# A DiT layer, from its first norm to its feed-forward: a fourth up tile in the norm's freed PSUM banks, and a written order of convolutions and operands

## The chip, the cores and the metric

The kernel runs on one core of a Trainium2 chip (trn2). The metric is the device time of one execution in microseconds (us), from the first to the last instruction of the core; where a number of runs is given, it is their median. Engines are named as in the profile: PE is TensorE's matmul (PEld its weight loads), DVE is VectorE, ACT is ScalarE, POOL is GpSimd, SP is SyncE, which here only issues DMAs (SPq).

## The reference, cut to what matters

One layer of a diffusion backbone over 1024 latent tokens and 256 context tokens, model width 1024, in fp32. Two attentions are merged, then comes a norm, then a feed-forward with a depthwise convolution of width 3 along the tokens, then a second norm. The change lies between the first norm and the feed-forward:

```python
x = _layer_norm(DEEPNORM_ALPHA * x + gate1 * y, ln1_g[l], ln1_b[l])
h = x * (1.0 + scale2) + shift2
y = _conv_ffn(h, w_up[l], conv_w[l], conv_b[l], w_down[l])
x = _layer_norm(DEEPNORM_ALPHA * x + gate2 * y, ln2_g[l], ln2_b[l])

def _conv_ffn(h, w_up, conv_w, conv_b, w_down):
    u = h @ w_up                      # 1024 -> 2 * 2816
    u = depthwise_conv3(u, conv_w) + conv_b
    gate, val = jnp.split(u, 2, axis=-1)
    return (jax.nn.silu(gate) * val) @ w_down
```

## The kernel before, in words

Activations lie transposed: 128 channels on the partitions, the tokens along the row. Every fp32 operand is split into a high part (a cast, on ScalarE) and a low part (the remainder, on VectorE or GpSimd), and a product is three matmuls: high-high, high-low, low-high (`mm3`, L87 to L90). `split` is L77 to L85; so nearly all casts show as L80 and nearly all weight remainders as L85, and `sub`'s differences as L1074.

**The first norm** works in three token ranges, `LN1_S`: tokens 0 to 511, 512 to 767, 768 to 1023. For each range `ln_steps` sums over the channels with small matmuls into a PSUM tile `sml`, spreads the result with another, and then, per channel block f of eight, applies it (L1050, L1052) and calls `emit1`: an affine step on ScalarE into the operand tile `B{f}_{half}` (its high part) and into a full value v, and the remainder into B's low part. B is the moving operand of the feed-forward's first matmuls.

**PSUM** has eight banks of 512 fp32 words per partition. The pool `ps3` has three `big` tiles of two banks each (1024 tokens) and two `sml` tiles of one bank. A pool is replaced by the next one bank by bank, as their readers end.

**The up tiles.** The 2816 + 2816 columns are 22 tiles j, each with a gate half (gv 0) and a value half (gv 1) of 128 channels. The first NCL = 3 tiles are direct products: u{gv}_{j} is 8 channel blocks x 3 matmuls x the tokens (`up_mm`, L1259 on). Tiles 3 to 21 use a form with seven products of half size (`up_tile`): A11, S2, S1, S3, A12, S4, A22, each 4 x 3 matmuls of 512 columns, with sums of the weights (`wsums`, GpSimd) and of the activations (`build`) as operands. `build(k)`, for k of 0 to 3, makes differences t13, t24 of the values (VectorE and GpSimd) and splits them into T13 and T24, high and low. `prods` says which product uses which: S2 needs T2 and A22 T4, both from T24; S1 and S3 need T1 and T3 from T13; A11, A12 and S4 use B itself.

**A direct tile's end.** `conv3` (L1229 on) convolves one half from PSUM into SBUF: a scaled copy on ScalarE (L1230), two shifted multiply-adds on VectorE (L1231, L1233); only then are the two banks free. Then silu of the gate half (L1283, ScalarE) and `gated`: a product (L1242) and an add (L1243) on VectorE, and stores to DRAM (`td`) on the SP queue (L1244 to L1246). The gate half c0 lies in one of two fixed slots `cs`; the value half c1 takes a slot from the free list.

**The free list.** `ht` takes the first slot of `hfree`, `hput` appends slots to its end, at the moment at which the program text is traced; the wait for the slot's last reader, a DMA included, becomes a wait of the instruction that writes the new tile first.

**The order.** TensorE is in an order written by hand (`tc.manual_schedule` over PE, entered ahead of this part and left at the kernel's end). The other engines' orders are chosen by the language's scheduler, by the order of the text among what its own model finds ready. Small steps are queued in `pend` with a due time and called by `tick` between matmuls; `drain` calls the rest.

Before the change three tiles (0,0), (0,1), (1,0) start in the three `big` buffers, range by range behind the norm (L1289 to L1296). Then the 16 steps of the four builds are put into `pend` at 2400 each, `up_conv(0)`, `up_conv(1)`, `up_conv(2)` follow (the missing half of tile 1 and both of tile 2 take a `big` buffer as one comes free), `drain` calls what is left of the builds, and the pool is replaced by `ps3u` with eight single banks. `up_tile(3)` takes four of them in the order of `PSU`.

Of the kernel before, what the change touches and what calls it, by code (L numbers as in the profile page):

```python
# [7 lines left out]
F32 = mybir.dt.float32  # L8
# [30 lines left out]
LN2_D = 5000.0, 4000.0, 2500.0, 1500.0, 700.0  # L39
LN2_E = 3500.0, 3000.0, 1500.0, 800.0, 500.0  # L40
NCL = 3
BLD = 2400.0
LN2_S = slice(0, 512), slice(512, 768), slice(768, 1024)
S1 = 0, 1
KVB = 2
# [22 lines left out]
def layer_kernel(  # L68
# [66 lines left out]
    def hput(*names):  # L135
        for n in names:
            hfree.append(hslot.pop(n))
# [735 lines left out]
    za = tc.alloc_tile_pool(name="za", bufs=1, side="right", reuse_waits="tile")  # L873
    wq = tc.alloc_tile_pool(name="wq", bufs=1, side="right", reuse_waits="tile")
    ps3 = tc.alloc_tile_pool(name="ps3", bufs=1, space=PSUM, reuse_waits="tile")

    hfree += [(za, f"Z{n}") for n in range(16)]

# [4 lines left out]
        return ps3.tile([P, T], F32, tag="big", name=name, bufs=3)  # L883

    def sml(name, w=512):
        return ps3.tile([P, w], F32, tag="sml", name=name, bufs=2)

    def weight(src, nm, n=8, tag="w", he=None, le=None, rtag="raw"):
        if rtag:
# [215 lines left out]
    def build(k):  # L1105
        (b11, b21), (b12, b22) = [[z[:, a] for a in (0, 1)] for z in (zt_[k, 0], tp["v", k])]
        st = {}

        def parts(a, e):
            for p in "hl":  # L1110
                tp[a + p, k] = ht(f"T{a}{p}_{k}", (P, 2, HALF), R32)
            nc.scalar.copy(tp[a + "h", k], st[a])
# [12 lines left out]

        return [s1, s2, lambda: parts("13", nc.vector), lambda: parts("24", nc.vector)]
# [145 lines left out]
    def up_conv(j):  # L1272
        cv = []
        for gv in (0, 1):
            up_mm(j, gv, [hsl(0), hsl(1)])
            if gv == 0:
                hslot[f"c0_{j}"] = pool, tag = cs[j % 2]
                t = pool.tile([P, T], F32, tag=tag, name=f"c0_{j}", bufs=1)
            else:
                t = ht(f"c1_{j}")  # L1280
            conv3(t, ups.pop((j, gv))[0], gv * NF + j)
            cv.append(t)
        nc.scalar.activation(cv[0], cv[0], AF.Silu)  # L1283
        gated(j, *cv)
        hput(f"c1_{j}")

    up_weights(1, 0, 1)
    up_weights(1, 1, 1)
    for j, gv in ((0, 0), (0, 1), (1, 0)):  # L1289
        up_start(j, gv)  # L1290
    for si, s in enumerate(LN1_S):
        drain((len(LN1_S) - 1 - si) * (KT + 3))
        for j, gv in ((0, 0), (0, 1), (1, 0)):
            up_mm(j, gv, [s])
            if s.stop == T:
                ups[j, gv][2].add(HALF)  # L1296
    cs = [hfree.pop(0) for _ in range(2)]
# [5 lines left out]
    hput(*[f"B{k}_1" for k in range(4)])  # L1303


    ps3.release()
    ps3 = tc.alloc_tile_pool(name="ps3u", bufs=1, space=PSUM, reuse_waits="tile")

    ubanks = list(PSU)

    def bank(name):
        n = ubanks.pop(0)
        ubanks.append(n)
        return ps3.tile([P, HALF], F32, tag=f"u{n}", name=name)

    for n in range(8):
        ps3.tile([P, HALF], F32, tag=f"u{n}", name=f"u{n}")

    def wload(j):
        wraw[j] = [post.tile([P, 8, P], F32, tag="raw", name=f"ru{gv}_{j}", bufs=3) for gv in (0, 1)]  # L1320
        for gv in (0, 1):
            nc.sync.dma_start(wraw[j][gv], w_up[2 * j + gv])
# [13 lines left out]
    def pairs(j, *names):  # L1336
        for n in names:
            if (j, n) not in wsrc:
                continue
            pool, tag = ((wq, "w"), (post, "wd"))[npair[0] % 2]  # L1340
            npair[0] += 1
            t = wtile[j, n] = pool.tile([P, 2, HALF], R32, tag=tag, name=f"w{n}_{j}", bufs=4)
            split(wsrc.pop((j, n)), t[:, 0], t[:, 1], nc.scalar, getattr(nc, UE[list(prods).index(n)]))

    def prod(j, n, o, start, stop):
        w = wtile.pop((j, n))
        for k in range(4):
            c = slice(k * P, (k + 1) * P)
            mm3(o, (w[:, 0, c], w[:, 1, c]), opnd(prods[n], k), start and k == 0, stop and k == 3, not start)
            tick(HALF / 0.8)  # L1350

    def add(o, p, q, e=nc.vector):
        e.tensor_tensor(out=o, in0=p, in1=q, op=ALU.add)

    lohalf, hihalf = slice(0, HALF), slice(HALF, T)

    def up_tile(j):
# [7 lines left out]
        nc.scalar.copy(pe, a)  # L1365
# [368 lines left out]
```

## Time and profile before

| | |
|---|---|
| median of 3 runs | 1618.45 us (1617.1 to 1619.27) |
| the profiled execution: span | 1618.4 us |
| TensorE busy (matmuls) | 1545.6 us, 95% |
| VectorE / ScalarE / GpSimd busy | 1199.0 / 816.8 / 746.4 us |
| mean granted TensorE clock | 0.987 |
| the stretch from 949.3 to 1029.0 us | 79.7 us, TensorE busy 67.07, clock 0.89 |

The profiled execution's own time is its span; nothing else lies around it. A row of the windows gives a stretch and, for each engine, busy time and number of instructions, then the clock that TensorE was granted. A row of the waits reads "who waited, at which tile and line, <- for what: total us, times, longest". In order of time a row is start, length, engine, line, operation, out<-in, and, in brackets, idle time of the engine before it and what ended it. Matmuls are pipelined: their listed lengths overlap, and the distance between starts is what one costs.

### The profile page before, as it was taken

To read this page: it belongs to the slowest core of one execution; us is meant where nothing else is said; L and a number is where in the kernel's file an instruction comes from. 1 tells how busy PE (TensorE), PEld (TensorE's weight loads), DVE (VectorE), ACT (ScalarE), POOL (GpSimd) and SP (SyncE) were. 2 spreads that over 40 slices of the span, in tenths; PEclk is the share of its full clock that TensorE was granted. 3 is DMA by queue.
4 is the path that set the end of the run, shared out by engine and by line. 5 is a ranking of instruction groups with operands and counts; after the bars stand their busy time and mean duration, and the time that the engine had idled before them with its cause. 6 is when DMAs were issued, how large, how long until landed. Compare 5 with 4: busy or idle time off the path is not lost.

```text
span 1618.4 us, 22204 instructions
## 1 busy us (share of the span) xinstructions
PE 1545.6 (95%) x7748; PEld 1283.5 (79%) x7748; DVE 1199.0 (74%) x1764; ACT 816.8 (50%) x1455; POOL 746.4 (46%) x731
## 2 busy tenths in 40 slices
PE   6999999999999999999999988999999999999987
PEld 5878788888877887777788876888888888888877
DVE  7797646538887777888765786588888788658883
ACT  5422122458887667788332563444444444436542
POOL 0583302526666556555333444566667764111131
PEclk9999999999999999999999999999999999999997
DMA  9695662322246655520540313123334447996711
GB/s 377 218 322 179 212 203 85 124 72 60 63 132 146 148 126 129 119 63 19 196 169 18 109 46 116 66 105 104 117 105 118 115 119 202 342 268 228 230 64 53
DMA packets 112369, 230.00 MB, mean 142 GB/s; under 512 B 12961, under 2 KB 27809, under 8 KB 112161
## 3 DMA queue, kind: packets, MB, share of 16 engines
q1 hardware_dynamic: 96816, 198.93, 36.6%
q0 software_dynamic: 10400, 20.19, 8.1%
q10 hardware_dynamic: 5040, 9.46, 1.6%
q8 instruction: 61, 1.00, 0.2%
q14 instruction: 52, 0.42, 0.1%
HBM read 177.35 MB, written 65.86 MB: 150 GB/s over the span
## 4 chain that ended last, share of the span: by engine, by line
PE 78%; DVE 9%; ACT 4%; issue 4%; POOL 3%; DMA 2%; SPq 0%; DVEq 0%; ACTq 0%; POOLq 0%
PE ptr L529 5%; PE p L88 4%; PE p L89 4%; PE p L90 3%; PE g L88 3%; PE g L89 3%; PE g L90 3%; PE b L90 3%; PE b L89 3%; PE b L88 3%; PE c L88 2%; PE c L89 2%; PE c L90 2%; PE d L89 2%; PE d L90 2%
## 5 line engine op out<-in xcount | busy, mean ns | idle before, releaser
L539 DVE TENSOR_TENSOR ptl<-ptr,pth 128x512 fp32r<-128x512 f32 x188 | 124.8, 685 | 27.9 <-ACT pth L538 25.2
L529 PE MATMUL ptr<-ident,p 128*128 128x128 f32 x816 | 126.5, 278 | 10.1 <-DVE ptl L539 7.7
L538 ACT CAST pth<-ptr 128x512 fp32r<-128x512 f32 x188 | 106.5, 588 | 56.4 <-PE ptr L529 32.6
L85 DVE TENSOR_TENSOR ld<-rd,hd 128x1024 fp32r<-128x1024 f32 x77 | 94.2, 1241 | 51.1 <-ACT hd L80 49.0
L424 ACT ACTIVATE p<-p,nm 128x1024 f32<-128x1024 f32 (+2 forms) x128 | 125.4, 982 | 10.9 <-DVE p L457 10.1
L529 PEld LDWEIGHTS ptr<-ident,p 128*128 128x128 f32 x816 | 93.7, 140 | 40.1 <-DVE ptl L539 13.4
L80 ACT CAST hd<-rd 128x1024 fp32r<-128x1024 f32 x77 | 79.3, 1051 | 81.7 <-PE p L90 51.1
L550 PE MATMUL av<-pth,VT 128*128 128x512 f32 x236 | 104.6, 443 | 1.0 <-ACT avs L556 0.5
L88 PE MATMUL p<-hd 128*128 128x512 f32 x264 | 103.2, 391 | 0.0
L90 PE MATMUL p<-hd,ld 128*128 128x512 f32 x264 | 102.7, 389 | 0.0
L89 PE MATMUL p<-ld,hd 128*128 128x512 f32 x264 | 102.7, 389 | 0.0
L88 PE MATMUL g<-hh,whg 128*128 128x512 f32 x256 | 99.9, 390 | 0.0
L90 PE MATMUL g<-hh,wlg 128*128 128x512 f32 x256 | 99.8, 390 | 0.0
L551 PE MATMUL av<-ptl,VT 128*128 128x512 f32 x236 | 97.7, 414 | 2.0 <-POOL ptl L85 1.9
L89 PE MATMUL g<-hl,whg 128*128 128x512 f32 x256 | 99.6, 389 | 0.0
L85 POOL TENSOR_TENSOR wlg<-wg,whg 128x512 fp32r<-128x512 f32 x32 | 45.1, 1415 | 109.9 <-ACT whg L80 109.9
L457 DVE TENSOR_SCALAR_CACHE_REDUCE p<-s,cvt,nmc 128x1024 f32<-128x1024 f32 x64 | 84.4, 1339 | 12.4 <-PE s L413 12.0
L412 PE MATMUL s<-KL,q 128*128 128x512 f32 (+2 forms) x192 | 76.1, 396 | 2.9 <-ACT p_x L424 2.0
L186 DVE CUSTOM_DVE_ANT_0 wml<-wml,sc,bmc 128x1024 f32<-128x1024 f32 x32 | 45.0, 1418 | 39.7 <-DMA wml<-in_wmodT_dram 38.2
L82 POOL TENSOR_SCALAR pth<-prw 128x512 fp32r<-128x512 f32 x48 | 31.1, 647 | 88.3 <-ACT prw L535 62.7
L413 PE MATMUL s<-KL,q 128*128 128x512 f32 (+2 forms) x192 | 71.7, 373 | 0.0
L80 ACT CAST wA<-ru 128x512 fp32r<-128x512 f32 x57 | 35.5, 623 | 71.5 <-PE d L90 34.1
(420 smaller groups left out, 5022.9 us busy)
## 6 DMA issues: line engine op xcount, KB each, us to landing
wml<-in_wmodT_dram SPq DMA_DIRECT2D x48, 512.0 KB
ru<-in_w_up_dram SPq DMA_DIRECT2D x38, 512.0 KB
rd<-td SPq DMA_DIRECT2D x55, 256.0 KB
rd<-sd SPq DMA_DIRECT2D x44, 256.0 KB
rd<-in_w_dn_dram SPq DMA_DIRECT2D x33, 256.0 KB
wm<-in_wmodT_dram SPq DMA_DIRECT2D x16, 512.0 KB
wg<-in_w_g_dram SPq DMA_DIRECT2D x32, 256.0 KB
sgd<-sg ACTq DMA_DIRECT2D x32, 256.0 KB
```

What stands on the lines that cost most here:

```text
L80: nc.scalar.copy(hi, src)
L85: lo_eng.tensor_tensor(out=lo, in0=src, in1=hi.bitcast(F32), op=ALU.subtract)
L88: nc.tensor.matmul(ps, a[0], b[0], start=start, stop=False, skip_group_check=resumed)
L89: nc.tensor.matmul(ps, a[0], b[1], start=False, stop=False, skip_group_check=resumed)
L90: nc.tensor.matmul(ps, a[1], b[0], start=False, stop=stop, skip_group_check=resumed)
L424: nc.scalar.activation(p, s, AF.Exp, bias=nm[:, h:h + 1], scale=scale, accum_out=sm[:, h:h + 1])
L457: nc.vector.tensor_scalar(out=p, in0=o, scalar1=self.qscale(nqs)[:, hs] if self.br else -1.0, scalar2=self.other[:, hs], op0=ALU.mult, op1 ...
L529: nc.tensor.transpose(tr[:, h * P:(h + 1) * P], self.pslice(h, n), ident)
L538: nc.scalar.copy(hi, tr)
L539: nc.vector.tensor_tensor(out=lo, in0=tr, in1=hi.bitcast(F32), op=ALU.subtract)
L550: nc.tensor.matmul(self.av, v, hi, start=first, stop=False)
L551: nc.tensor.matmul(self.av, v, lo, start=False, stop=self.left == 0)
```

## The change

1. The two `sml` tiles move into a pool of their own, `ps3s`. Ahead of the last token range the norm's queued steps are drained, that pool is released, and a pool `ps3c` with one two-bank tile takes its place: u1_1, the value half of tile 1. Its first two ranges are issued on TensorE ahead of the last range of all tiles, and then its last range behind those of the other three.
2. `build`, the convolutions, the gating of tiles 0 and 1, the weights of tile 2, the load, sums and first four operand pairs of tile 3 are written out in one order, in a region in which VectorE, ScalarE and GpSimd each keep the order of the text. Where the region's instructions fall among those outside it stays the scheduler's. The `pend` entries of the builds and their constant `BLD` go; `up_conv(2)` stays behind the region.
3. For tile 3 alone the products run A11, S1, S3, S2 instead of A11, S2, S1, S3.
4. The order of the eight banks in `PSU` is 4, 5, 6, 7, 0, 1, 2, 3 instead of 6, 7, 2, 3, 4, 5, 0, 1.

```diff
-PSU = 6, 7, 2, 3, 4, 5, 0, 1
+PSU = 4, 5, 6, 7, 0, 1, 2, 3
...
     ps3 = tc.alloc_tile_pool(name="ps3", bufs=1, space=PSUM, reuse_waits="tile")
+    ps3s = tc.alloc_tile_pool(name="ps3s", bufs=1, space=PSUM, reuse_waits="tile")
...
-    for j, gv in ((0, 0), (0, 1), (1, 0)):
+    early = (0, 0), (0, 1), (1, 0)
+    for j, gv in early:
         up_start(j, gv)
     for si, s in enumerate(LN1_S):
         drain((len(LN1_S) - 1 - si) * (KT + 3))
-        for j, gv in ((0, 0), (0, 1), (1, 0)):
+        if s.stop == T:
+            ps3s.release()
+            ps3s = tc.alloc_tile_pool(name="ps3c", bufs=1, space=PSUM, reuse_waits="tile")
+            ups[1, 1] = ps3s.tile([P, T], F32, tag="big4", name="u1_1"), upw.pop((1, 1)), set()
+            early += (1, 1),
+            up_mm(1, 1, LN1_S[:si])
+        for j, gv in early:
             up_mm(j, gv, [s])
...
-    for k in range(4):
-        pend += [(BLD, fn) for fn in build(k)]
-    for j in range(NCL):
-        up_conv(j)
-    drain()
...
+    def conv_in(j, gv):
+        if gv == 0:
+            hslot[f"c0_{j}"] = pool, tag = cs[j % 2]
+            t = pool.tile([P, T], F32, tag=tag, name=f"c0_{j}", bufs=1)
+        else:
+            t = ht(f"c1_{j}")
+        conv3(t, ups.pop((j, gv))[0], gv * NF + j)
+        cv[j, gv] = t
+
+    def gate_out(j):
+        g, v = cv.pop((j, 0)), cv.pop((j, 1))
+        nc.scalar.activation(g, g, AF.Silu)
+        gated(j, g, v)
+        hput(f"c1_{j}")
+
+    with tc.manual_schedule(engines={mybir.EngineType.DVE, mybir.EngineType.Activation, mybir.EngineType.Pool}):
+        for k in (0, 1):
+            built[k][0]()
+            built[k][1]()
+        conv_in(0, 0)
+        up_weights(2, 0)
+        conv_in(0, 1)
+        built[0][2]()
+        built[0][3]()
+        gate_out(0)
+        up_weights(2, 1)
+        built[2][0]()
+        built[2][1]()
+        conv_in(1, 0)
+        built[1][2]()
+        built[1][3]()
+        wload(NCL)
+        wsums(NCL, tm)
+        built[2][2]()
+        built[2][3]()
+        conv_in(1, 1)
+        built[3][0]()
+        built[3][1]()
+        pairs(NCL, "A11")
+        built[3][2]()
+        pairs(NCL, "S1")
+        gate_out(1)
+        built[3][3]()
+        pairs(NCL, "S3", "S2")
+    up_conv(2)
+    drain()
...
-        prod(j, "S2", b, True, True)
-        add(ve, b, pe)
+        if j > NCL:
+            s2()
         prod(j, "S1", c, True, True)
         nc.scalar.copy(uv[:, hihalf], c)
+        if j == NCL:
+            s3()
+            s2()
         pairs(j, "A12", "S4", "A22")
...
-        prod(j, "S3", d, True, True)
-        add(uv[:, hihalf], d, uv[:, hihalf])
+        if j > NCL:
+            s3()
...
-    wload(NCL)
-    wsums(NCL, tm)
-    pairs(NCL, "A11", "S2", "S1", "S3")
```

`s2` and `s3` are the two products with the additions that follow them, as before. `built[k]` holds the four steps of `build(k)`: t13, t24 (which returns two slots), the split of T13, the split of T24.

More of the change, by code (lines that the diff above doesn't have):

```diff
@@ L885, in sml @@
     def sml(name, w=512):
-        return ps3.tile([P, w], F32, tag="sml", name=name, bufs=2)
+        return ps3s.tile([P, w], F32, tag="sml", name=name, bufs=2)
     def weight(src, nm, n=8, tag="w", he=None, le=None, rtag="raw"):
@@ L1292, in layer_kernel @@
         drain((len(LN1_S) - 1 - si) * (KT + 3))
-        for j, gv in ((0, 0), (0, 1), (1, 0)):
+        if s.stop == T:
[5 more added lines that the diff above has]
+        for j, gv in early:
             up_mm(j, gv, [s])
             if s.stop == T:
-                ups[j, gv][2].add(HALF)
-    cs = [hfree.pop(0) for _ in range(2)]
-    for k in range(4):
-        pend += [(BLD, fn) for fn in build(k)]
-    for j in range(NCL):
-        up_conv(j)
-    drain()
[L1303 to L1317, printed above, removed]
+                ups[j, gv][2].update((0, HALF))
     def wload(j):
@@ L1343, in pairs, with bank @@
             split(wsrc.pop((j, n)), t[:, 0], t[:, 1], nc.scalar, getattr(nc, UE[list(prods).index(n)]))
+    cs = [hfree.pop(0) for _ in range(2)]
+    built = [build(k) for k in range(4)]
+    cv = {}
+    def conv_in(j, gv):
[42 more added lines that the diff above has]
+    drain()
+    hput(*[f"B{k}_1" for k in range(4)])
+    ps3s.release()
+    ps3.release()
+    ps3 = tc.alloc_tile_pool(name="ps3u", bufs=1, space=PSUM, reuse_waits="tile")
+    ubanks = list(PSU)
+    def bank(name):
+        n = ubanks.pop(0)
+        ubanks.append(n)
+        return ps3.tile([P, HALF], F32, tag=f"u{n}", name=name)
+    for n in range(8):
+        ps3.tile([P, HALF], F32, tag=f"u{n}", name=f"u{n}")
     def prod(j, n, o, start, stop):
@@ L1365, in up_tile, with s2, s3 @@
         nc.scalar.copy(pe, a)
-        prod(j, "S2", b, True, True)
-        add(ve, b, pe)
+        def s2():
+            prod(j, "S2", b, True, True)
+            add(ve, b, pe)
+        def s3():
+            prod(j, "S3", d, True, True)
+            add(uv[:, hihalf], d, uv[:, hihalf])
+        if j > NCL:
+            s2()
         prod(j, "S1", c, True, True)
         nc.scalar.copy(uv[:, hihalf], c)
+        if j == NCL:
+            s3()
+            s2()
         pairs(j, "A12", "S4", "A22")
```

1 line of the change is left out of this document (removed).

## The prediction

> **What bounds the kernel now.** First the page, for the span and the busiest engine; then the table of windows between the end of the norm's second token range and the second tile of the seven-product form; then the waits of TensorE there; then its instructions.
>
> ```profile
> span 1618.4 us, 22204 instructions
> PE 1545.6 (95%) x7748; PEld 1283.5 (79%) x7748; DVE 1199.0 (74%) x1764; ACT 816.8 (50%) x1455; POOL 746.4 (46%) x731
> ```
>
> The windows (columns: stretch, its length, then PE, PE's weight loads, DVE, ACT and POOL busy with their instructions, TensorE's clock, DMA share, GB/s), and the waits of TensorE from 949 on:
>
> ```profile
> 940.70:949.30 8.60, 8.60 (x75) 8.60 (x74) 8.60 (x13) 8.53 (x17) 6.76 (x7) 1.00 0.37 122
> 949.30:1029.00 79.70, 67.07 (x300) 55.59 (x299) 52.45 (x52) 32.00 (x38) 30.57 (x22) 0.89 0.21 73
> 999.70:1018.10 18.40, 11.44 (x37) 8.51 (x36) 8.16 (x9) 4.89 (x7) 1.29 (x1) 0.72 0.24 85
> 1029.00:1048.10 19.10, 19.10 (x86) 15.79 (x86) 14.84 (x16) 9.25 (x13) 10.65 (x7) 1.00 0.33 110
> ```
>
> ```profile
> PE b L88 <- ACT T24h L1112: 6.5, 1, 6.5
> PE u L88 <- DVE c L1233: 3.0, 1, 3.0
> PE u L89 <- DVE B L1074: 1.4, 1, 1.4
> PE u L89 <- POOL B L1074: 1.3, 1, 1.3
> PE b L89 <- DVE T24l L1074: 0.5, 1, 0.5
> ```
>
> TensorE is busy 95% of the span and bounds it, so only a stretch where it stands still can be won. Before 949.3 and after 1029.0 its row is full at clock 1.00; between them it is not. There it has 72 matmuls of 256 columns (the last token range of three up tiles), 144 of 512 (the tiles written u1_1, u0_2, u1_2) and 84 of 512 (tile 3). The last window gives 19.1/84 = 0.227 us for one of 512, the first about 8.6/72 = 0.12 us for one of 256. So the work is 8.6 + 32.7 + 19.1 = 60.4 us in 79.7: 19.3 us are lost. The five waits make 12.7; the rest is the half clock after them:
>
> ```profile
> 965.27 0.47 PE L88 MATMUL u<-B,hwu 128*128 128x512 f32 x1 [2.96 <-DVE c L1233]
> ...
> 966.97 0.63 PE L88 MATMUL u<-B,hwu 128*128 128x512 f32 x1
> 967.39 0.63 PE L89 MATMUL u<-B,hwu 128*128 128x512 f32 x1
> ```
>
> Starts lie 0.42 us apart instead of 0.227 soon after a stall of 2.96. In the third window above, with the 6.5 us stall, 18.4 us hold 37 matmuls (8.4 us) and 7.0 of waits; the other 3.0 are the price in clock of one long stall (clock 0.72 in that row).
>
> The longest wait is the one to understand (the chain of waits, start and length):
>
> ```profile
> 1005.71 0.33 SPq L1244
> ...
> 1006.62 3.22 DMA td<-c
> ...
> 1009.93 1.05 ACT T24h L1112
> ```
>
> T24h of block 3 is written into the SBUF slot of c1_2 (the convolved value half of up tile 2). It must wait until the gating of that tile has ended (second add, 1006.4) and its store to td has read c1_2: 3.5 us from the add to the cast.
>
> **The change, part by part.** The durations used below: groups of VectorE from 960 to 1007 (busy, mean ns, idle before), three of its passes in order of time, one group of GpSimd, two instructions of ScalarE.
>
> ```profile
> L1231 DVE SCALAR_TENSOR_TENSOR c<-u,cvt,c 128x1023 f32<-128x1023 f32 x6 | 7.7, 1276 | 8.9 <-ACT c L1230 8.9
> ...
> L1242 DVE TENSOR_TENSOR c<-c,c 128x1024 f32<-128x1024 f32 x3 | 4.7, 1582 | 0.0
> ...
> L1074 DVE TENSOR_TENSOR t<-v,t 128x512 f32<-128x512 f32 x2 | 2.3, 1174 | 0.0
> ...
> L1074 DVE TENSOR_TENSOR t<-z,t 128x512 f32<-128x512 f32 x1 | 0.7, 674 | 0.0
> ```
>
> ```profile
> 1004.46 1.22 DVE L1242 TENSOR_TENSOR c<-c,c 128x1024 f32<-128x1024 f32 x1
> 1005.72 0.69 DVE L1243 TENSOR_TENSOR c<-c 128x512 f32<-128x512 f32 x1
> 1006.33 0.68 DVE L85 TENSOR_TENSOR wS<-s,wS 128x512 fp32r<-128x512 f32 x1
> ```
>
> ```profile
> L1074 POOL TENSOR_TENSOR s<-ru 128x512 f32<-128x512 f32 x2 | 2.6, 1294 | 0.0
> ```
>
> ```profile
> 1000.11 1.20 ACT L1230 ACTIVATE c<-u,cvt 128x1024 f32<-128x1024 f32 x1
> ...
> 1002.53 0.59 ACT L1365 COPY pv<-a 128x512 f32<-128x512 f32 x1 [0.71 <-PE a L90]
> ```
>
> *The fourth tile.* u1_1 takes the two banks of the norm's small tiles, whose last reader is long done, and its first two ranges run ahead of the last range: 24 x 0.227 + 24 x 0.12 = 8.3 us of TensorE work from 949.3 to 957.6. The operands B that the last range waited for end on VectorE here:
>
> ```profile
> 952.91 1.82 DVE L1074 TENSOR_TENSOR B<-v,B 128x256 fp32r<-128x256 f32 x2
> ```
>
> that is at 954.7, so the waits of 1.3 and 1.4 go. Price: 24 matmuls of 512 become 48 of 256, 24 x 0.24 - 24 x 0.227 = 0.3 us. The last range now takes four groups of 24 x 0.12 = 2.9: they end at 960.5, 963.4, 966.3, 969.1. u0_2 needs the banks of u0_0: ScalarE's 1.2 and VectorE's two passes of 1.27 after 960.5 end near 964.4, before 969.1. The wait of 3.0 goes. Then u0_2 runs to 980.0, u1_2 to 990.9, and tile 3 could start there instead of 999.7, and tile 4 at 949.3 + 60.4 + 0.3 = 1010.0 instead of 1029.0: 19.0 us, if nothing were late next.
>
> *What is late next: VectorE.* The block now fixes its order. After the first convolution it stands at the low half of weight (2,0), whose buffer frees when u0_1 ends, 966.3. From there to the second add of tile 1's gating I count 11 full-width two-operand passes (2 weight halves, T13l of blocks 0 to 3, T24l of 0 to 2, 2 gate products), 8 convolution passes (those of u1_0, u0_1, u1_1, and of u0_2, which is outside the block and which A11 needs since its bank is u0_2's), and 9 half-width ones (2 adds, 5 differences, A11, S1). 11 x 1.22 + 8 x 1.27 + 9 x 0.68 = 29.7 us; neighbours overlap by some 0.07 each (the pass at 1005.72 ends at 1006.41, the next starts at 1006.33), so 27.7. The means of 1582 and 1174 against 1220 and 674 show what GpSimd at work beside such a pass costs: 3 x 0.36 + 2 x 0.50 = 2.1 us in the old stretch. Seven GpSimd passes (three differences, the four weight sums) lie beside this list; I take 2.5, from 0 to 9 (all seven shut VectorE out for the 1.29 of the last row). For heads of the queue that wait I take 2 (0 to 5): the four sums stand ahead of block 3's difference on GpSimd, so T13l of block 3 waits for one such pass and a cast of 1.05, less the little that VectorE has in hand. So the gating of tile 1 ends at 966.3 + 27.7 + 2.5 + 2 = 998.5, from 994.0 to 1008.
>
> *One slot in a ring.* Free SBUF slots are taken from the front of a list and returned to its end. Behind the pair for the gate halves nine are free when the block begins, and c1_0 takes the first. Blocks 0 and 1 return 4, T of block 0 takes 4, tile 0's gating returns c1_0's slot behind 8, block 2 returns 2 behind it. T of blocks 1 and 2 takes the 8, so c1_1 gets c1_0's slot again. Block 3 returns 2; its T13 takes block 2's, tile 1 returns the slot, T24 takes block 3's; c1_2 gets the slot and returns it, and pv3, tile 3's two-part buffer, is the next to be taken (the four B halves are returned behind). So: end of tile 1's gating, 3.5 until its store has read c1_1, then the convolution of u1_2 into c1_2 and gating 2, then 3.5 again, then ScalarE's copy of A11's result into pv3, and A12 may not add to that bank before the copy. In the old trace convolution to second add took 6.3 (1000.1 to 1006.4), with one half-width pass between. So A12 starts at 998.5 + 3.5 + 6.3 + 3.5 + 0.6 = 1012.4. TensorE itself: A11 waits for u0_2's convolution and its own low half, which the written order reaches 4 to 5 us before 998.5, so it starts near 994 rather than 990.9; A11, S1, S3, S2 take 4 x 12 x 0.227 = 10.9, with slow clock to about 1008. It then stands some 4 us. ScalarE's copy holds nothing that is needed earlier: S1's evacuation and the casts are ready before it. After the stall: 3 x 12 x 0.227 + 3.0 for the clock, so tile 4 starts at 1023.6 instead of 1029.0. The 6.5 us wait for T24h itself is gone (block 3's T24 takes the slot of z3_0), but the same store, of the same tile, is waited for three products later.
>
> From tile 4 on I cost the edit at nothing: 19.1 us at clock 1.00 per tile, the weights of tile 4 are made during the stall. The new bank order ends the last tile on 4 to 7, and the next product starts on 4 and 5, which tile 21 empties two products before its end. **Sum:** 19.3 us lost before; afterwards 0.3 for the split matmuls and 13.6 for stalls and clock, so -5.4, and 1618.4 becomes 1613.0. The page's span, 1618.4, and the median, 1618.45, agree, so I take nothing between them.
>
> [...] The old trace has this pair:
>
> ```profile
> 983.53 1.75 POOL L1074 TENSOR_TENSOR s<-ru,s 128x512 f32<-128x512 f32 x1
> ```
>
> ```profile
> 984.06 2.31 DVE L1242 TENSOR_TENSOR c<-c,c 128x1024 f32<-128x1024 f32 x1
> ```
>
> A gate product of 1.22 alone takes 2.31 beside a GpSimd sum. [...]
>
> **The rivals.** *The slot does not bind.* If pv3 got a free slot, at most A11's 3 us and 3.0 of clock were left: gain 13 to 19, time 1599 to 1605. For it: three waits surely go. Against: the old T24h shows that a reused slot waits for the store. Chance 0.08.
>
> *Contention eats it.* All seven passes shut VectorE out: 9 instead of 2.5 moves the gating, and with it A12, by 6.5: 1619.5, within 3 us of no change. Chance 0.18.
>
> *The store queue, slower.* The stores of gating 1 and 2 go through SP, in order, where the loads of tile 4 and 5's weights also queue:
>
> ```profile
> 990.12 11.82 SPq L1322 DMA_DIRECT2D ru<-in_w_up_dram  x2
> ```
>
> SP stood there nearly 12 us for a free raw-weight buffer, with the stores of tile 2 behind it. If such a load now comes ahead of gating 1's or 2's stores, each us that it holds them past their time is one us at the end. Break-even is at 5.4 us of holding, and at the row's full 11.8 us the time is 1613.0 + 11.8 = 1624.8. Against: in the old order the buffer came free at 1001.9, before the stores were due (1005.7). Chance 0.12.
>
> *Not what it says:* nothing in the edit lets the scheduler undo the fixed order, but u0_2's convolution lies outside it; put last on VectorE, A11 starts near 1002 and the stall before A12 shrinks by as much: the time stays near the forecast, and this has no case of its own.
>
> **How the numbers follow.** Forecast 1613.0, chance 0.62, its own range 1608 to 1617 (gating 1 ending from 994.0, and the half-width pass of 0.6 beside gating 2 away, to 1002). Faster by over 0.2% (3.2 us, about what a measurement of this kernel can tell from no change): 0.56 of the forecast's 0.62 and the first rival, 0.64. Within: the other 0.06 and the second rival, 0.24. Slower: 0.12. The range 1603.5 to 1620.0 leaves out most of the first rival and of the third.
>
> **What would show it.** Right: no wait of TensorE on B or on L1233 between 950 and 970, u1_1 in the window before 958; VectorE nearly full from 966 to 1000; ScalarE's copy into pv released by a DMA from c, near 1012, and A12 of tile 3 waiting for that copy. Wrong: tile 4 (forecast: 1023.6) starting near 1010, or A12 not waiting; a wait of tile 3 for weights; a stall in the last range. If VectorE's two-operand passes there average over 1.6 us, the second rival holds; if SP's wait for L1322 stands ahead of L1246, the third.

## The result: 3.2 us faster, and the profile after

The changed kernel takes 1615.23 us (median of 22 runs) against 1618.41 for the kernel before on the same chip: ratio 0.998, 95% interval 0.997 to 0.9989, so 3.2 us faster (1.8 to 4.9). Predicted were 1613.0 and 5.4. The page of the profiled execution:

```profile
span 1613.3 us, 22253 instructions
PE 1542.9 (96%) x7772; PEld 1280.9 (79%) x7772; DVE 1203.9 (75%) x1764; ACT 815.7 (51%) x1455; POOL 752.3 (47%) x731
```

Its span is 5.1 us below that of before, but not all of this is the change. I cut both traces at the first matmul of an up tile (u), at tile 4's A11, and at the first matmul of the down projection (p). From u to tile 4 it is 109.5 us before (919.51 to 1029.04) and 106.0 after (920.93 to 1026.97): 3.5 us. From tile 4 to p it is 342.7 in both. The stretch behind p took 246.6 us in the profiled execution of before and 243.6 in that of after, with the same work, so 3.0 us of the difference in span are a matter of that execution. In what follows "the stage" is u to tile 4's A11, and 1.42 us (920.93 - 919.51) are taken off a time of after to set it beside the forecast.

The windows of after, cut at the same places of the work as those of before (length, PE, its weight loads, DVE, ACT, POOL, then TensorE's clock, DMA share, GB/s), and TensorE's waits in the first of them:

```profile
950.70:1027.00 76.30, 66.02 (x325) 55.24 (x324) 57.79 (x52) 31.51 (x38) 33.29 (x22) 0.91 0.23 76
1001.90:1021.10 19.20, 11.19 (x38) 8.37 (x37) 14.54 (x14) 4.45 (x7) 10.37 (x7) 0.76 0.40 135
1027.00:1046.10 19.10, 19.10 (x86) 15.82 (x85) 14.65 (x16) 9.15 (x13) 9.90 (x7) 1.00 0.33 111
```

```profile
PE a L87 <- ACT pv L1417: 7.4, 1, 7.4
PE a L87 <- DVE c L1233: 2.2, 1, 2.2
PE d L89 <- DVE wS L84: 0.6, 1, 0.6
```

The waits on B and on the convolution L1233 of the old list are gone, and tile 4's row is what it was: 19.10 at clock 1.00. What was 79.7 us long is 76.3 now, with 60.7 us of work (60.4 and 0.3 for the split matmuls): 15.6 are lost instead of 19.3, 10.2 of them in these three waits; the other 5.4 I put down to half clock behind them (the clock was 0.52 from 994.52 to 997.92 and 0.50 from 1015.80 to 1021.50). The old list's longest wait was 6.5 us in S2, then tile 3's second product; the new one is 7.4 us at A12, its fifth. The second window shows it: 19.20 us with 38 matmuls and clock 0.76, as in the old row (0.72).

The chain in front of A12, all engines in order of time, other lines left out:

```profile
999.55 0.69 DVE L1243 TENSOR_TENSOR c<-c 128x512 f32<-128x512 f32 x1
...
1000.45 0.39 SPq L1246 DMA_DIRECT2D td<-c  x1
...
1003.75 1.21 ACT L1230 ACTIVATE c<-u,cvt 128x1024 f32<-128x1024 f32 x1 [1.89 <-DMA td<-c]
...
1008.53 2.05 DVE L1242 TENSOR_TENSOR c<-c,c 128x1024 f32<-128x1024 f32 x1
1009.46 2.24 POOL L1074 TENSOR_TENSOR s<-ru,ru 128x512 f32<-128x512 f32 x1
...
1010.62 1.63 DVE L1243 TENSOR_TENSOR c<-c 128x512 f32<-128x512 f32 x1
...
1011.67 1.70 POOL L1074 TENSOR_TENSOR s<-s,ru 128x512 f32<-128x512 f32 x1
1012.32 0.37 SPq L1246 DMA_DIRECT2D td<-c  x1
...
1013.40 0.62 ACT L79 CAST wS<-s 128x512 fp32r<-128x512 f32 x1 [8.44 <-POOL s L1074]
...
1015.16 0.58 ACT L1417 COPY pv<-a 128x512 f32<-128x512 f32 x1 [1.14 <-DMA td<-c]
```

Gating 1's second add (L1243) ends at 1000.24; SP issues its store; ScalarE may write the convolved u1_2 (c1_2) into the slot at 1003.75, released by the DMA from c: 3.51 us. Gating 2 ends at 1012.25, 8.5 us after that convolution began; its store is issued at 1012.32, and ScalarE's copy into pv comes at 1015.16, again released by the DMA from c. A12 starts at 1015.80. Note the cast at 1013.40: it stands ahead of the copy in ScalarE's queue and waits 8.44 us for GpSimd, but without it the copy would still have waited for the DMA, as its own bracket (1.14) says. That cast comes back below. The two rows of GpSimd (1009.46 and 1011.67) lie beside the product and the add of gating 2, which take 2.05 and 1.63 instead of 1.22 and 0.69.

### The profile page after: what moved, and what is told of

Its sections match the earlier page's. It is cut to its first block, busy times and chain, and to the rows that moved or that the text cites. A ratio compares the mean times of both kernels' runs of the same rounds, so it can differ in the third digit from the quotient of the medians.

```text
span 1613.3 us, 22253 instructions
## 1 busy us (share of the span) xinstructions
PE 1542.9 (96%) x7772; PEld 1280.9 (79%) x7772; DVE 1203.9 (75%) x1764; ACT 815.7 (51%) x1455; POOL 752.3 (47%) x731
## 4 chain that ended last, share of the span: by engine, by line
PE 68%; DVE 12%; DMA 7%; ACT 4%; issue 4%; POOL 3%; SPq 0%; ACTq 0%; DVEq 0%; POOLq 0%
PE ptr L528 5%; PE p L88 3%; PE p L89 3%; PE p L87 3%; PE b L89 3%; PE b L88 3%; PE b L87 3%; DMA wml<-in_wmodT_dram 2%; PE av L549 2%; PE a L87 2%; PE s L411 2%; PE a L88 2%; PE a L89 2%; PE c L87 2%; PE av L550 2%
## 5 line engine op out<-in xcount | busy, mean ns | idle before, releaser
L537 ACT CAST pth<-ptr 128x512 fp32r<-128x512 f32 x188 | 106.5, 588 | 56.5 <-PE ptr L528 32.8
L456 DVE TENSOR_SCALAR_CACHE_REDUCE p<-s,cvt,nmc 128x1024 f32<-128x1024 f32 x64 | 84.4, 1339 | 12.3 <-PE s L412 12.0
L87 PE MATMUL a<-B,wA 128*128 128x512 f32 x152 | 61.0, 401 | 9.6 <-ACT pv L1417 7.4
```

The costliest lines, as they stand in the source:

```text
L87: nc.tensor.matmul(ps, a[0], b[0], start=start, stop=False, skip_group_check=resumed)
L456: nc.vector.tensor_scalar(out=p, in0=o, scalar1=self.qscale(nqs)[:, hs] if self.br else -1.0, scalar2=self.other[:, hs], op0=ALU.mult, op1 ...
L537: nc.scalar.copy(hi, tr)
```

## The experiments

Two theories. **The slot:** A12 waits because pv3 is given the slot of c1_0, c1_1 and c1_2, whose last store ends late; with another slot the wait goes. **The backlog:** VectorE, with GpSimd beside it, is late with everything, and a wait that is taken away comes back at the next product. Each kernel was timed against the kernel before on the same chip. The chips differ between sets of runs (the kernel before took 1617.1 to 1619.9 us there), so rows are compared by their ratios, and "below before" in the text is what the ratio makes of 1618.4 us. "Stage" and "u to p" (109.5 and 452.3 before) are from the one profiled execution of each.

| kernel | median us | ratio, 95% interval | stage us | u to p us |
|---|---|---|---|---|
| after | 1615.23 | 0.998 [0.997, 0.9989] | 106.0 | 448.8 |
| e1_pv3_slot | 1611.07 | 0.9955 [0.9937, 0.9973] | 100.5 | 443.2 |
| e2_c1_and_pv3 | 1611.37 | 0.995 [0.9932, 0.9968] | 100.6 | 443.3 |
| e3_tile4_alone | 1614.36 | 0.9968 [0.9955, 0.9981] | 103.7 | 446.4 |
| e4_order_alone | 1617.75 | 0.999 [0.9976, 1.0003] | 106.5 | 449.2 |
| e5_pv3_act_order | 1610.83 | 0.9954 [0.9939, 0.9969] | 97.4 | 442.6 |
| e6_parts_early | 1610.81 | 0.9959 [0.9947, 0.9972] | 100.0 | 442.7 |
| e7_no_sums | 1614.5 | 0.9978 [0.9964, 0.9992] | 103.7 | 446.4 |
| e8_all | 1608.14 | 0.9942 [0.9925, 0.996] | 95.2 | 442.0 |
| e9_all_dve_order | 1606.61 | 0.9924 [0.9907, 0.9941] | 91.4 | 439.8 |
| e10_no_act_order | 1610.19 | 0.9949 [0.9929, 0.9969] | 98.4 | 441.1 |
| e11_tile4_and_slot | 1611.15 | 0.9961 [0.9946, 0.9975] | 98.6 | 441.3 |

What u to p loses against 452.3 runs up to 3 us ahead of what the medians lose (e6: 9.6 against 6.6), and 4.6 for e11; the single execution of before was a long one, 1.8 us above its median by the share of time outside the span that is given below. So the medians carry the verdicts, and the traces the causes. The stage ends at tile 4's A11, and what tile 4 gives back lies outside it: from there to p it takes 342.7 us before, after and in eight of the experiments, but 345.2 in e5, 346.9 in e8 and 348.4 in e9.

### e1: pv3 in another slot

```diff
     hput(*[f"B{k}_1" for k in range(4)])
+    hfree.append(hfree.pop(0))
```

> The change, with one line more: pv3 of tile 3 takes the slot of a B half that is free, and c1_2's slot goes to the end of the list. Theory (the reused slot holds A12): the copy of A11's result follows A11, so the 7.4 us wait of A12 and the 2.5 to 3 us of clock behind it go; A12 follows S2, tile 4 starts about 10 us earlier than in the change, time about 1605.5, 0.992 of the kernel before. Rival (VectorE's backlog holds tile 3 anyway): another wait of 4 us or more in A12, S4 or A22, time 1611 or above. In both the 2.2 us wait of A11 stays.

The ratio is 0.9955, 7.3 us below before and some 4 below the changed kernel; the stage lost 5.5 more. ScalarE copies into pv at 1003.59 and A12 follows S2. So the reused slot was what held A12. But there is a new wait, at S4, all engines in order of time:

```profile
1003.59 0.57 ACT L1418 COPY pv<-a 128x512 f32<-128x512 f32 x1
...
1006.55 1.29 POOL L1074 TENSOR_TENSOR s<-ru 128x512 f32<-128x512 f32 x1 [3.62 <-DMA ru<-in_w_up_dram]
...
1011.78 0.62 ACT L79 CAST wS<-s 128x512 fp32r<-128x512 f32 x1 [7.61 <-POOL s L1074]
...
1012.30 0.58 ACT L1430 COPY uv<-c 128x512 f32<-128x512 f32 x1
```

S4 adds to the bank from which uv is copied. That copy needs nothing but S1's result (S3 had followed S1 at 1000.49, 12 us before), but it stands behind a cast of tile 4's weight sum, and the cast waits 7.61 us for GpSimd, which itself waited for its weights to land (3.62, DMA ru). The backlog theory is right in this part: the wait came back, smaller, two products on, though through ScalarE's queue and the weights of the next tile rather than VectorE's list.

### e2: the second gating too in a slot of its own

The edit is in up_conv, which only tile 2 still goes through.

```diff
             else:
+                hput(*[f"B{k}_1" for k in range(4)])
+                hfree.append(hfree.pop(0))
                 t = ht(f"c1_{j}")
...
-    hput(*[f"B{k}_1" for k in range(4)])
```

> As the run with pv3's own slot, and c1_2 too gets the slot of a B half, so the convolution of u1_2 no longer waits for the store of tile 1. Theory: that convolution starts near 992 instead of 1003.8, but nothing on TensorE waits for it, so the time is that of the first run within 1 us, about 1605.5. Rival: its two passes and the gate product, some 4.5 us of VectorE, come ahead of the low halves that S1, S3 and S2 need, and the time is 2 to 4 us above the first run.

0.995, with e1 within the interval, and the same stage. S4 waits 4.14 us for the same copy behind the same cast, so what the earlier slot for c1_2 could give may have gone into that wait. It adds nothing to e1, and whether c1_2's slot is worth anything without ScalarE's queue stays open here.

### e3 and e4: the fourth tile alone, the written order alone

e3 is the kernel before with u1_1 in the norm's freed banks ahead of the last range and PSU as changed, the builds' steps at 1200 and no written block. e4 is the changed kernel without the fourth early tile:

```diff
-PSU = 4, 5, 6, 7, 0, 1, 2, 3
+PSU = 6, 7, 4, 5, 2, 3, 0, 1
...
-            ups[1, 1] = ps3s.tile([P, T], F32, tag="big4", name="u1_1"), upw.pop((1, 1)), set()
-            early += (1, 1),
-            up_mm(1, 1, LN1_S[:si])
...
+    up_mm(1, 1, [hsl(0), hsl(1)])
     cs = [hfree.pop(0) for _ in range(2)]
```

> The kernel before with the fourth tile and the new bank order alone: no written order on VectorE, ScalarE and GpSimd, products of tile 3 in the old order A11, S2, S1, S3, and the steps of the builds due at 1200 instead of 2400 so that all are called ahead of the return of c1_2's slot. Theory: the waits on B and on the convolution go (5.7 us and some 3.5 of clock); T24 of block 3 no longer takes c1_2's slot; c1_2 lies in a slot free early, so gating 2 can begin when u1_2 ends (992) and the copy into pv3 is ready near 1005; S2, second in the old order, waits 2 to 4 us for T24 of block 3. Time 1606 to 1611, below the change. Rival (the written order is what gains): S2's wait for T24 stays near the old 6.5 us, time 1613 to 1617.

> The change without the fourth tile: u1_1 runs in a big buffer behind the last range, as in the kernel before; the written order and the product order S1, S3, S2 stay; banks 6, 7, 4, 5, 2, 3, 0, 1. Theory: the waits on B and on the first convolution come back (5.7 us and their clock), A11 starts near 1000 as in the kernel before, gating 1 still ends near 999 because VectorE has the same list, so the slot chain ends near 1013 and A12 waits only 1 to 3 us; the time is within 2 us of the change, 1613 to 1617: what the fourth tile gains is given back at A12. Rival (the two parts add up): 1619 or above, since without the fourth tile its 9 us are missing.

TensorE's waits in e3, then in e4:

```profile
PE u L88 <- DVE c L1234: 4.7, 1, 4.7
PE a L88 <- ACT pv L1374: 3.2, 1, 3.2
PE u L90 <- DVE lwu L85: 1.0, 1, 1.0
```

```profile
PE a L87 <- ACT pv L1410: 8.0, 1, 8.0
PE u L88 <- DVE B L1073: 1.4, 1, 1.4
```

The fourth tile alone takes 0.9968, 5.2 us, no less than the whole change as far as the overlapping intervals tell; the order alone 0.999, with 1 inside the interval. The parts don't add. What the earlier steps of the builds give by themselves was not run, so their share of e3's 5.2 us is open. In e4 the waits on B are back (1.4 here, and 1.3 for the part that GpSimd makes), and A12 waits 8.0 for the same copy into pv, where 1 to 3 were expected, since A11 began at 995.46 and not near 1000: the written order alone runs into the store, too. e3 took the time of its rival, but not for the rival's reason: S2 doesn't wait. In e3 u0_2 waits 4.7 for its convolution, since VectorE, with no written order, makes the T halves first; that delays A11 to 1002.51, but VectorE isn't idle from 956 to 963, and A12 waits only 3.2 for the same copy.

### e6: the T halves of blocks 0 and 1 ahead of the first convolution

In the changed kernel VectorE stands idle from 956.2 to 963.1, because the written order puts the convolution of u0_0, whose banks TensorE fills only by 961.9, ahead of T halves that could be made at once. VectorE's first pass of that convolution in the changed kernel:

```profile
963.13 1.28 DVE L1231 SCALAR_TENSOR_TENSOR c<-u,cvt,c 128x1023 f32<-128x1023 f32 x1 [6.93 <-ACT c L1230]
```

```diff
         for k in (0, 1):
             built[k][0]()
             built[k][1]()
+        built[0][2]()
+        built[0][3]()
+        built[1][2]()
+        built[1][3]()
         conv_in(0, 0)
         up_weights(2, 0)
         conv_in(0, 1)
-        built[0][2]()
-        built[0][3]()
...
-        built[1][2]()
-        built[1][3]()
```

> The changed kernel, with the high and low halves of T13 and T24 of blocks 0 and 1 moved ahead of the first convolution in the written order; pv3 keeps its slot. VectorE stood idle for 6.93 us there (956.2 to 963.1). Theory (VectorE's list dates the store that A12 waits for): four passes of 1.22 leave the list, so the second add of gating 1 ends 4.9 us earlier (995.3 instead of 1000.24), A11 no longer waits for the convolution of u0_2 and starts at about 992.3, and A12 and tile 4 start 4.9 us earlier than in the changed kernel, with a wait of 4 to 5.5 us still in front of A12 for ScalarE's copy into pv; the time is 4 to 5 us below the changed kernel, 7 to 8 below the kernel before. Rival (the end of the stage is set by something else: tile 4's weights, ScalarE's queue, the store itself): A11 moves, A12 and the time stay within 1 us of the changed kernel.

VectorE in e6, and TensorE's two waits in tile 3:

```profile
955.79 1.21 DVE L1074 TENSOR_TENSOR T13l<-t,T13h 128x1024 fp32r<-128x1024 f32 x1
...
960.29 1.21 DVE L1074 TENSOR_TENSOR T24l<-t,T24h 128x1024 fp32r<-128x1024 f32 x1
```

```profile
PE a L87 <- ACT pv L1417: 3.0, 1, 3.0
PE a L87 <- DVE c L1233: 3.0, 1, 3.0
```

The four passes (the first and the last stand here) fill the gap. Gating 1 ends at 995.85 instead of 1000.24 (4.0 us earlier, counted from u), and the stage is 6.0 us shorter than in the changed kernel; 0.9959, 6.6 us below before, a little less than the 7 to 8 expected. The wait in front of A12 falls from 7.4 to 3.0, below the 4 to 5.5 expected: counted from u, gating 2 ended 4.8 us earlier (at 1007.05, where it was 1012.25) and S2 only 0.4. One point failed: A11 still waits for the convolution of u0_2. That lies outside the written block, and its last pass, planned among the others, went to 993.47, behind the product of gating 1.

### e7: without GpSimd's sums

For tiles 3 and 4 the products S1 to S4 take raw quarters of the weights, so the four sums are left out, and the kernel no longer computes the layer.

```diff
+        if j <= NCL + 1:
+            wsrc.update({(j, "S1"): a21, (j, "S2"): a22, (j, "S3"): a11, (j, "S4"): a12})
+            return
```

> The changed kernel without GpSimd's four weight sums for tiles 3 and 4: the products S1 to S4 of these two tiles take the raw quarters of the weights in place of the sums, so this part of the computation is left out; every cast, low half and matmul stays. Theory (GpSimd beside VectorE's full-width passes stretches them): T13l and T24l of block 2, 2.31 and 2.31 in the changed kernel, go back to 1.22, and so do the product and the add of gating 2, 2.05 and 1.63 to 1.22 and 0.69. The second add of gating 1 ends about 2.2 us earlier, gating 2 takes 6.7 to 7.5 instead of 8.5, and A12 and tile 4 start 3 to 4.5 us earlier than in the changed kernel; the time is 3 to 4.5 below it. Rival (only the length of VectorE's queue counts, and its passes are long for another reason): the passes keep 2.31, and the time stays within 1 us of the changed kernel.

VectorE's passes, and GpSimd's:

```profile
984.18 2.31 DVE L1074 TENSOR_TENSOR T13l<-t,T13h 128x1024 fp32r<-128x1024 f32 x1
986.42 1.21 DVE L1074 TENSOR_TENSOR T24l<-t,T24h 128x1024 fp32r<-128x1024 f32 x1
...
1007.14 1.23 DVE L1242 TENSOR_TENSOR c<-c,c 128x1024 f32<-128x1024 f32 x1
1008.40 0.69 DVE L1243 TENSOR_TENSOR c<-c 128x512 f32<-128x512 f32 x1
```

```profile
983.21 2.20 POOL L1074 TENSOR_TENSOR t<-v 128x512 f32<-128x512 f32 x1 [8.72 <-DVE T13l L1074]
993.74 4.48 POOL L1074 TENSOR_TENSOR t<-z,t 128x512 f32<-128x512 f32 x1 [8.32 <-DVE t L1074]
```

The stretching comes from GpSimd: T24l of block 2 takes 1.21 instead of 2.31, gating 2's product and add 1.23 and 0.69 instead of 2.05 and 1.63. T13l keeps its 2.31, because block 3's difference now lies beside it (983.21). The stage gains 2.3, the time 3.6 against before, hardly more than the changed kernel's 3.2: less than the 3 to 4.5 expected. Gating 2 ended 2.9 us earlier, counted from u, but its store then took 4.3 us to read the slot instead of 2.9, and A12 waits 7.5 as before.

### e5, e8, e9, e10: the causes taken away together

e5 is e1 with ScalarE's order written in tile 3: the copies into pv and uv ahead of the casts of tile 4. e8 is e5 and e6 with A11 in u0_1's bank and its low half made earlier. e9 is e8 with VectorE's adds, too, ahead of the low halves of tile 4. e10 is e8 without e5's order. A part of e9's edit against the changed kernel:

```diff
-PSU = 4, 5, 6, 7, 0, 1, 2, 3
+PSU = 0, 1, 6, 7, 4, 5, 2, 3
...
+        pairs(NCL, "A11")
         built[2][2]()
...
+        own = ExitStack()
+        if j == NCL:
+            own.enter_context(tc.manual_schedule(engines={mybir.EngineType.Activation, mybir.EngineType.DVE}))
         prod(j, "A11", a, True, True)
         nc.scalar.copy(pe, a)
...
         pairs(j + 1, "A11")
+        if j == NCL:
+            pairs(j + 1, "S2")
```

> The kernel of e1_pv3_slot (pv3 in another slot), with ScalarE's order written for the first part of tile 3: the copy of S1's result into uv comes ahead of the casts of tile 4's sums, where in e1_pv3_slot it stood behind a cast that waited 7.61 us for GpSimd. Theory (the second stall of e1_pv3_slot is only a place in ScalarE's queue): the 3.04 us in front of S4 go. What is late next is the add of S3's bank on VectorE, which stands behind the low half of tile 4's S2; that half waits for the same GpSimd sums and ended at about 1013.0 in e1_pv3_slot, while A22 could start at 1012.4, so A22 waits about 1.3. Tile 4 starts 1.7 to 3.0 us earlier than in e1_pv3_slot, and the time is some 10 to 12 us below the kernel before. Rival (VectorE's backlog or the weights of tile 4 hold the end of tile 3, whatever ScalarE's order): tile 4 starts within 0.5 us of e1_pv3_slot's, 9 us below the kernel before.

> The changed kernel with all the moves: pv3 in another slot, ScalarE's order in tile 3, the T halves of blocks 0 and 1 ahead of the first convolution, and A11 in the bank of u0_1 with its weight's halves made ahead of block 2's T halves. Theory (each stall has the cause that was named, and they lie in a row): A11 follows u1_2 at once, S1, S3, S2, A12 and S4 follow without a wait of over 1 us, A22 waits 0 to 1.5, and the stage from the first u matmul to tile 4 takes 90.5 to 93 us against 109.5 before and 106.0 in the changed kernel; the time is 16 to 19 us below the kernel before. Rival (VectorE's work of the block is the bound, and a wait goes only to come back at the next product): the stage takes 96 us or more, the time is at most 13 us below the kernel before. Second rival (what is won is given back behind tile 4, where weights and stores come earlier than their engines are free): the stage is short, the time is not, and new waits stand in tiles 4 to 21.

> The kernel of e8_all, with VectorE's order written too in the first part of tile 3: the adds of S3's and S2's results come ahead of the low halves of tile 4's A11 and S2. In e8_all A22 waited 3.41 us for the first of these adds, which stood behind the low half of tile 4's S2 (1011.33 to 1012.54), itself 4.30 us in wait for a cast and GpSimd's sums. Theory: A22 follows S4 at once, and the stage from the first u matmul to tile 4 takes 91 to 92.5 us instead of 95.2; the low half of tile 4's S2 is ready 2 us before it is used. The wait of 2.25 at tile 4's own A22 stays or grows by 1 at most; the time is 2 to 4 us below e8_all, 12 to 16 below the kernel before. Rival (the chain of GpSimd's sums, casts and low halves is the bound of this stretch, and takes back at tile 4 what tile 3 gains): the stage is as short, but tile 4's A22 waits 4 to 6, and the time is within 1 us of e8_all.

> The kernel of e8_all without ScalarE's written order in tile 3 (pv3 in another slot, T halves of blocks 0 and 1 early, A11 in u0_1's bank). Theory (ScalarE's queue is the next stall once the slot is free): A11 to A12 follow u1_2 without a wait of over 1 us, and S4 waits 3.5 to 5 for the copy of uv behind a cast that waits for GpSimd; A22 follows at once, and in tile 4 no wait is over 1. The stage takes 95 to 97 us against 95.2 in e8_all; the time is 10 to 13 us below the kernel before. Rival (the wait at S4 was a matter of VectorE's backlog, which is 4.9 us shorter here): S4 waits less than 1.5, and the stage takes 91 to 93 us.

In e5 the wait at S4 is gone and the stage is 97.4, but tile 4's own A22 waits 2.2 for VectorE's add, and the median is e1's (ratios 0.9954 and 0.9955). In e10 S4 waits for the copy into uv, as ScalarE's queue says, a little over the 3.5 to 5 expected, and with half clock behind it (starts 0.43 us apart from 1012.38) the stage is 98.4; the time is 8.3 us below before, where 10 to 13 were expected:

```profile
PE c L87 <- ACT uv L1430: 5.0, 1, 5.0
```

In e8 no product of tile 3 up to S4 waits over 1 us, A22 waits 3.4 for the add that stands behind a low half of tile 4's S2, and the stage is 95.2, not the 90.5 to 93 of the theory; the time is 9.4 us below before, not 16 to 19. In e9 that wait is gone too, and the stage is 91.4; the waits that are left in tile 4 are

```profile
PE c L87 <- ACT uv L1433: 2.0, 1, 2.0
PE d L87 <- DVE uv L1406: 1.7, 1, 1.7
PE a L87 <- ACT pv L1421: 1.0, 1, 1.0
```

together 4.7 us, where e8 had one of 2.25. So both theories held a part: each stall had the cause that was named and went with it, and the chain behind them (raw weights land, GpSimd's four sums, casts, low halves) then asks for 1.5 of the 3.8 us back in tile 4 (24.7 us long in e9, 23.2 in e8, 19.0 in the changed kernel). e9 has the lowest ratio here, 0.9924 [0.9907, 0.9941]: 12.3 us below before and some 9 below the changed kernel. Its interval overlaps that of e8, so the gain over e8 is shown by the traces and not by the times.

### e11: e3 with pv3 in another slot

The line of e1 added to e3, so no written order at all.

> The kernel of e3_tile4_alone (the fourth tile and the new banks, without the written order), with pv3 taken from another slot of the free list. In e3_tile4_alone A12 waited 3.20 us for ScalarE's copy into pv, and that copy 8.91 us for the store of the convolved value half. Theory (the reused slot is the cause there too): the wait in front of A12 is gone; S4 then waits 0 to 4 for the copy into uv, which stands in ScalarE's queue behind casts of tile 4's sums. From the first u matmul to tile 4 it takes 99 to 103.7 us instead of 103.7, and the time is 6 to 10 us below the kernel before. Rival (in that order of work the slot is free in time and something else dates the copy): A12 waits as before, and the time is 5 to 6 below the kernel before.

The wait in front of A12 is gone, and no product of tile 3 waits: A11 at 1000.93, tile 4 at 1019.97, 19.04 us. ScalarE's copy into uv, at 1009.29, follows S1's end; tile 4's sums were early enough. The time is 6.3 below before (0.9961), at the low end of what was expected, though u to p lost 10.9; its interval overlaps that of e3, so the gain over e3 is shown by the trace and not by the times.

## Why the prediction was right, and where it was not

The kind of outcome and its cause were right: the three early waits go, VectorE then dates the gating of tiles 1 and 2, and A12 waits for the copy into pv through a reused slot and its store. Point by point, in the clock of before:

- *The fourth tile, the last range.* No wait there; TensorE is busy for 42.00 of 42 us from 949 to 991 at clock 1.00. Right.
- *VectorE's list.* Forecast 998.5, measured 998.8. The total was right and its parts were not. I put in 2.5 for contention and 2 for heads of the queue that wait. The queue never waited (from the low half at 967.59 of after's trace to the add at 999.55 one pass follows another), and four passes took 2.31 or 2.29 instead of 1.22: 4.3 us. Two errors cancelled, which was luck.
- *A11.* Forecast near 994, measured 993.1, for the reason given.
- *The store.* 3.5 forecast, 3.51 and 2.91 measured.
- *Gating 2.* Here the forecast failed: "In the old trace convolution to second add took 6.3", and it took 8.5 (1003.75 to 1012.25). The low half of a weight was in front of it in the queue, and tile 4's sums, whose weights land at 1008.24, lie beside its product and add; e7, without them, has 1.23 and 0.69 there. So A12 was 2.0 us late (1014.4 against 1012.4): 2.2 in gating 2, less 0.6 in the store, and 0.3 in gating 1.
- *Behind A12.* Forecast 3 x 12 x 0.227 + 3.0 = 11.2 us to tile 4, measured 11.17. Tile 4 starts at 1025.6 instead of 1023.6, and 5.4 - 2.0 is, within 0.1, the 3.5 of the traces.
- *Span and median agree.* Wrong, and so is the sentence ahead of the prediction that nothing else lies around the span, though it did little: 1.7 to 2.2 us of the time lie outside the span in every run behind the prediction, 1.7 to 1.9 in those of the kernel before. So the profiled execution of before, with its span of 1618.4, was about 1.8 us above its median.

Of the rivals, "the slot does not bind" fell with e1. But its price was wrong in a way that matters: I gave 13 to 19 us for a free slot, and e1 gained 7.3. "The weights of tile 4 are made during the stall" was true of the changed kernel, and was the next stall once that one was short. Contention is real (4.3 us in the list, 1.8 in gating 2), though it didn't eat the gain. That all seven GpSimd passes shut VectorE out, 9 us, was my estimate (seven times 1.29), and no run shows it: in the changed kernel four passes took 1.07 to 1.09 longer, and the convolution passes beside GpSimd's of 987.87, 990.09 and 991.34 took 2.46 for two and 1.26, no longer than usual. By the sign that the prediction gave for this rival, it would have held: the eleven full-width two-operand passes from 967.59 to 999.52 average 1.61 us, a hair over 1.6. But 11 passes at 1.6 are only 4.2 us more than at 1.22, of which 2.5 were in the sum already, and the 2 us put in for heads of the queue that wait were not spent; so the sign was set far too low for a loss of 6.5 us, and gating 1 ended 0.3 us late. The store queue did no harm: the loads of the next weights were issued at 1004.26, behind gating 1's stores and 6 us ahead of gating 2's.

Where the gain of 19 us went: e3, e4 and e6 show that the written order is worth little as written, since it makes VectorE idle for 6.9 us at its head, and both parts run into the same store in front of A12. Without the slot (e1), without the idle time (e6) and without the two queues' order (e9), 12.3 us are there; the stage of e9, 91.4, is 0.9 us from the 90.5 that TensorE's own work would take (109.5 - 19.3 + 0.3), but 5.7 us come back behind it, in tile 4 (348.4 to p instead of 342.7).

## What to carry to other kernels

When a change takes waits away on the bounding engine, follow the next product's operands through every in-order queue and every reused buffer, down to who reads the buffer last: here a slot of a free list and its store took 7.4 us of the 12.7 that five waits had held. A hand-written order should begin with what is ready; e6 moved four passes and doubled what the change had won (3.2 to 6.6 us). And an evacuation that needs nothing but a finished product should not stand in a queue behind a cast of the next tile's weights: for such a copy S4 waited 3.04 us in e1 and 5.0 in e10.

## What the runs showed of the hardware

Passes of GpSimd and VectorE began by turns, 0.93 to 1.31 us apart, in the changed kernel (other engines left out):

```profile
983.47 2.20 POOL L1074 TENSOR_TENSOR s<-ru 128x512 f32<-128x512 f32 x1 [8.72 <-DVE T13l L1074]
984.44 2.31 DVE L1074 TENSOR_TENSOR T13l<-t,T13h 128x1024 fp32r<-128x1024 f32 x1
985.75 2.15 POOL L1074 TENSOR_TENSOR s<-s,ru 128x512 f32<-128x512 f32 x1
986.68 2.31 DVE L1074 TENSOR_TENSOR T24l<-t,T24h 128x1024 fp32r<-128x1024 f32 x1
987.87 2.27 POOL L1074 TENSOR_TENSOR s<-ru,ru 128x512 f32<-128x512 f32 x1
988.91 1.27 DVE L1231 SCALAR_TENSOR_TENSOR c<-u,cvt,c 128x1023 f32<-128x1023 f32 x1
```

T13l and T24l take 2.31 instead of 1.22, 1.09 us longer each, and GpSimd's sums 2.2 instead of 1.29: both lose. The convolution pass at 988.91, which reads u from PSUM and c from SBUF, takes its usual 1.27 beside a sum. In e7 the turns weren't even: GpSimd's difference took 4.48 us (row above, 993.74), while VectorE began and ended three passes of 1.21, 0.68 and 1.21.

Behind waits of about 3 us half clock did not follow the length of the wait. In each fence the first row is the matmul behind a wait, and the last two show the distance of starts soon after: 0.23 was full clock (1.00 from 1027.00 to 1046.10 of after), 0.43 half (0.50 from 966.50 to 968.00 of before and from 1015.80 to 1021.50 of after). TensorE in e8, e1 and e6:

```profile
1013.20 0.50 PE L87 MATMUL d<-T24h,wA 128*128 128x512 f32 x1 [3.41 <-DVE uv L1406]
...
1014.92 0.39 PE L88 MATMUL d<-T24l,wA 128*128 128x512 f32 x1
1015.15 0.40 PE L89 MATMUL d<-T24h,wA 128*128 128x512 f32 x1
```

```profile
1012.93 0.50 PE L87 MATMUL c<-B,wS 128*128 128x512 f32 x1 [3.04 <-ACT uv L1430]
...
1013.78 0.63 PE L87 MATMUL c<-B,wS 128*128 128x512 f32 x1
1014.21 0.63 PE L88 MATMUL c<-B,wS 128*128 128x512 f32 x1
```

```profile
1010.59 0.50 PE L87 MATMUL a<-B,wA 128*128 128x512 f32 x1 [2.96 <-ACT pv L1417]
...
1012.11 0.63 PE L87 MATMUL a<-B,wA 128*128 128x512 f32 x1
1012.53 0.63 PE L88 MATMUL a<-B,wA 128*128 128x512 f32 x1
```

After 3.41 us in e8 the starts stayed 0.23 apart; after 3.04 in e1 and 2.96 in e6 they went to 0.43, but 0.9 and 1.5 us after work had begun again. In before, behind the wait of 2.96 in the prediction's rows, the clock was 0.98 for 1.2 us (965.27 to 966.50) and 0.50 from there to 968.00. So waits of about 3 us cost next to nothing beyond themselves (A22 in e8 takes 2.87 us, a product at full clock 2.72), or 1.4 and 1.7 us (A12 in e6 4.08, S4 in e1 4.44); what decides between the two, these runs do not show. What makes the stretch behind p take 242.7 to 244.0 us in ten of the profiled executions and 246.6 to 247.3 in three (before, e10, e11), with a lower clock in the last stage (0.86 from 1550 to 1600 in before, 0.93 in after), stays open.
